# One core, a hybrid S5 and SSD layer: loads of the S5 output tied to gate tiles, and a place of its own for each S5 output block

## Chip, cores and metric

The kernel runs on one core of a Trainium2 chip. The metric is the time of one execution on the device, in microseconds (us). The five engines of the core are named as in the profile: PE (TensorE), DVE (VectorE), ACT (ScalarE), POOL (GpSimd) and SP (SyncE), which here issues all DMAs.

## What is computed

One layer of a streaming encoder, 1024 frames of 1024 channels, in float32. Cut to what matters here:

```python
hn   = rmsnorm(h, norm_w)
proj = hn @ w_in                                   # 1024 x (u | z_s5 | z_ssd | xBC | dt)
u_s5, z_s5, z_ssd, xBC, dt_raw = split(proj)

# S5 branch: 64 groups of 16 channels, 64 complex states each
y    = scan(u_s5) ... + D * u_s5
y    = gelu(y)                                     # "S5 output", Yd in the kernel
y    = y * sigmoid(y @ w_glu + b_glu)              # the GLU: needs all of y at once
y_s5 = y * silu(z_s5)

# SSD branch: 16 heads, state 128, in 8 steps of 128 frames
y    = ssd_chunked(silu(conv(xBC)), dt, A, B, C) + D * xs
g    = y * silu(z_ssd)
y_sd = g * rsqrt(mean(g*g over 256 channels) + EPS) * norm_w

h    = h + concat(y_s5, y_sd) @ w_out
h    = h + (p @ w_ple) * sigmoid(rmsnorm(h) @ w_gate)
out  = rmsnorm(h)
```

## The kernel before

Every large product works on tiles of 128 output channels by 1024 frames. A weight tile comes by one DMA into `wraw`, ACT casts it into `whi` (L138), POOL or DVE makes the remainder `wlo` (L141), and PE then does, for each of 8 slices of the inner dimension, three products (hi x hi, hi x lo, lo x hi) on two halves of 512 frames, so 48 matmuls a tile (`dense`, L162). These weight matmuls are the bulk of the work of PE.

The program order around the change is:

- projections of `u`, with the first parts of the S5 branch (a generator, `s5_chain`) pulled between;
- 16 convolution tiles and 4 gate tiles. The S5 branch goes on between them and ends with `s5_out`: eight blocks of eight channel groups. Block b needs its Toeplitz block `tp` (eight loads of 64 KB from `Kd`, L468), its inputs `ug` (one load from `Ud`, L399) and the rows `CAo` that DVE makes from `cb`. PE does 16 small products into two PSUM tiles, ACT puts the Gelu of each into SBUF (L508), and one DMA stores the block to `Yd` (L509). The loads of block b+1 are written ahead of the products of block b. `tp` and `ug` have two places each;
- 12 gate tiles (`z_tile`: a product, a Silu on ACT, a store to `Zd` in L846). The SSD chain (`ssd_chain`, steps k = 0 to 7) is pulled between and in the middle of them. Among the last eight of these tiles stand the 16 loads that bring the S5 output back as `m_0` to `m_7`, two for each (L874);
- the GLU: all eight `m` are split into hi and lo (L226 has the subtraction), then eight product tiles, each followed by a load of the gate `z` (L886) and the two multiplications; the SSD chain goes on;
- the output projection and what follows.

A step k of the SSD chain loads `csB` (decays, broadcast to 128 partitions, L605) and `cc` (L606), has 16 DVE operations for the decays (L618, eight and eight), and an exponential on ACT; matmuls on `csB` give the step's output; `ys` is multiplied with the gate block `zc` (L681) and squared; the squares are summed over partitions by matmuls with ones: ACT copies the hi part `nh` (L174), DVE subtracts for the lo part `nl` (L175), and PE does one matmul on each (L176, L177). Behind them stand the products with `BT` for the next state (L709) and the scores of the next step (L628).

Three things set the order. Engines execute their own instructions in order. The order in which the instructions of an engine stand is decided by a scheduler when the kernel is built, from the program's dependencies and its estimate of durations; a dependency can also be added by hand that holds for this order alone and puts no semaphore on the chip (`in_line`). And all DMAs stand in SP's queue in one order; besides what it needs, each waits for the DMA eight places ahead of it to have landed.

Of the kernel before, what the change touches and what calls it, by code (L numbers as in the profile page):

```python
# [8 lines left out]
F32 = mybir.dt.float32  # L9
F32R = mybir.dt.float32r  # L10
AF = mybir.ActivationFunctionType
ALU = mybir.AluOpType

P = 128
# [28 lines left out]
ZORD = list(range(8, 16)) + list(range(8))  # L43
# [16 lines left out]
def hybrid_layer(ctx: ExitStack, tc: tile.TileContext, xT, pT, w_in, w_dt, w_glu, w_out, w_gate, w_ple,  # L60
                 prm, cst, bst, cstt, crow, brow, out):
    nc = tc.nc
    V, S, G, T = nc.vector, nc.scalar, nc.gpsimd, nc.tensor
    dma = nc.sync.dma_start
# [34 lines left out]
    Yd = dram.tile([64, 8, 16, P], F32, tag="Yd", name="Yd")  # L99
# [10 lines left out]
    def psa():  # L110
        return ps_a.tile([P, 512], F32, tag="a", name="psa")

    def hf(t, i):
        return t[:, i * 512:(i + 1) * 512]
# [34 lines left out]
    def wnext(ahead=1):  # L149
        wfetch(1)  # L150
        w = wq.pop(0)
        wfetch(ahead)
        return w
# [10 lines left out]
    def dense(wt, rhs, nk=KT, cols=HALVES, bank=psd, mid=None):  # L164
        ps = [bank()[:, :x.stop - x.start] for x in cols]
        for k in range(nk):
            if mid is not None and k == nk // 2:
                mid()
            dense_k(ps, wt, rhs, k, nk, cols)
        return ps  # L170
# [26 lines left out]
    def in_line(ins):  # L197

        for a, b in zip(ins, ins[1:]):
            tc.add_manual_dep(b.ins, a.ins.name, mybir.DependencyInfo(mybir.DependencyClass.NoSync, mybir.DependencyReason.DATA),  # L200
                              reason="in line")

    def evac(ps, dst, func=AF.Copy):
        for h in range(2):
            S.activation(hf(dst, h), ps[h], func)


    def js(ap):
        return ap.rearrange("p (t j s) -> p t s j", j=8, s=16)
# [20 lines left out]
    def pull(gen, n=1):  # L230
        for _ in range(n):
            if next(gen, "end") == "end":
                return False
        return True
# [228 lines left out]
    def load_out(q4, b):  # L463
        cb = q4.tile([P, 2, 8, 16], F32, tag="cb", name="cb")
        dma(cb, crow[:, b])
        tp = q4.tile([P, 8, P], F32, tag="tp", name="tp")
        for s in range(8):
            dma(tp[16 * s:16 * s + 16],  # L468
                Kd[b].rearrange("(g h) c -> h g c", h=16)[:, :, 112 - 16 * s:240 - 16 * s])
        return cb, tp, load_u(q4, b)  # L470

    def s5_out(Er, Ei, wx, q4, ahead):
        with tc.tile_pool(name="q5", bufs=1, side="right") as q5:

            EO = q5.tile([P, 2, 8, 64], F32, tag="EO", name="EO")
            lo_, up = slice(0, 64), slice(64, P)
            for g2, src in enumerate((lo_, up)):
                for r, j, x, sign in ((lo_, 0, Er, 1.0), (lo_, 1, Ei, 1.0), (up, 0, Ei, -1.0), (up, 1, Er, 1.0)):
                    S.activation(EO[r, j, :, g2:64:2], x[src, J0 + 1:J0 + 9], AF.Copy, scale=sign)

            def rows(b, cb):

                CA = q5.tile([P, 8, 8, 16], F32, tag="CAo", name="CAo", bufs=2)
                t = q5.tile([P, 8, 8, 16], F32, tag="cat", name="cat")
                for j, dst in ((0, CA), (1, t)):
                    V.tensor_tensor(dst, cb[:, j, :, None, :].broadcast_to([P, 8, 8, 16]),
                                    EO[:, j, :, 8 * b:8 * b + 8].rearrange("p j g -> p g j")[:, :, :, None].broadcast_to([P, 8, 8, 16]),
                                    ALU.mult)
                V.tensor_tensor(CA.rearrange("p g j c -> p (g j c)"), CA.rearrange("p g j c -> p (g j c)"),
                                t.rearrange("p g j c -> p (g j c)"), ALU.subtract)  # L490
                return CA
            CA = rows(0, ahead[0][0])
            yield
            for b in range(8):
                _, tp, ug = ahead.pop(0)
                if b < 7:
                    ahead.append(load_out(q4, b + 1))
                    nxt = rows(b + 1, ahead[0][0])
                ysb = tp.rearrange("p (q g) c -> p q g c", g=2)
                for g2 in range(2):  # L500
                    yp = psa()
                    for q in range(4):
                        o = yp[:, q * P:(q + 1) * P]
                        g = 2 * q + g2
                        T.matmul(o, tp[:, g, :], ug[:, g, :], start=True, stop=False)  # L505
                        T.matmul(o, CA[:, g].rearrange("p j c -> p (j c)"), wx[:, 8 * b + g].rearrange("p r c -> p (r c)"), start=False, stop=True)  # L506

                    S.activation(ysb[:, :, g2, :].rearrange("p q (s j) -> p q s j", j=8), js(yp), AF.Gelu_apprx_tanh)  # L508
                dma(Yd[8 * b:8 * b + 8].rearrange("g t h c -> (t h) g c"), tp)  # L509
                CA = nxt  # L510
                yield

# [304 lines left out]
    for m in range(8):  # L817
# [5 lines left out]
        else:  # L823
            ps = dense(wnext(), xhl)
# [11 lines left out]
    def z_tile(m, mid=None):  # L836

        z = pz.tile([P, NT], F32, tag="z", name="z")
        ps = dense(wnext(), xhl, mid=mid)
        if m < 8:  # L840
            evac(ps, z, AF.Silu)
        else:
            zk = z.rearrange("p (k t c) -> p t k c", k=8, t=8)
            for h in range(2):
                S.activation(zk[:, 4 * h:4 * h + 4], ps[h].rearrange("p (t k c) -> p t k c", t=4, k=8), AF.Silu)
        dma(Zd[m], z)  # L846


    es_z = ExitStack()
    pz = es_z.enter_context(tc.tile_pool(name="pz", bufs=2))  # L850
    with tc.tile_pool(name="p3", bufs=2) as p3:
        at = {"c": 0, "z": 0}
        for c, n in zip(SEQ, PX):
            m = at[c]
            at[c] += 1
            if c == "c":
                conv_tile(m, p3)
            else:
                z_tile(ZORD[m])
            pull(s5, n)  # L860
# [6 lines left out]
    mt = [mpool.tile([P, NT], F32, tag=f"m_{m}", name=f"m_{m}") for m in range(8)]  # L867
    ssd = ssd_chain()
    for m, n in zip(range(NZ, 16), PZ):
        z_tile(ZORD[m], lambda: pull(ssd, n))  # L870

        for i in range(8)[m - NZ - 4:m - NZ - 3] if m >= NZ + 4 else ():
            for h2 in range(2):
                dma(mt[i][64 * h2:64 * h2 + 64].rearrange("p (t c) -> p t c", t=8), Yd[:, :, 2 * i + h2, :])  # L874
        pull(ssd, n)


# [2 lines left out]
    for m in range(8):  # L880
        ps = dense(wnext(), yhl, mid=lambda: pull(ssd, PG[m]))
# [3 lines left out]
        z = pz.tile([P, NT], F32, tag="z", name="z6")  # L885
# [9 lines left out]
    for m in range(8):  # L895
        dma(h_t[m], xT[m])
        ps = dense(wnext(), mhl, mid=lambda: pull(ssd, PO[m]))
# [8 lines left out]
    with tc.tile_pool(name="npool", bufs=1, side="right") as npool:  # L906
# [10 lines left out]
        for m in range(8):  # L917
            raw = npool.tile([P, NT], F32, tag="raw", name="m2raw", bufs=2).rearrange("p (k c) -> p k c", k=8)
            dma(raw, Sd[:, m].rearrange("k p c -> p k c"))
            t = npool.tile([P, NT], F32, tag=f"m2_{m}", name=f"m2_{m}")  # L920
# [6 lines left out]
    for m in range(8):  # L927
        ps = dense(wnext(1 if m < 7 else 0), m2hl)
# [29 lines left out]
    for m, cols in [(m, HALVES if m < GB else A2) for m in range(8)] + [(m, LASTC) for m in range(GB, 8)]:  # L958
# [9 lines left out]
        for i, c in enumerate(cols):  # L968
            n = c.stop - c.start
# [136 lines left out]
```

## Time and profile before

| | |
|---|---|
| Time, median of 3 runs | 994.84 us (993.02 to 996.24) |
| The profiled execution | 993.96 us, span 992.1 us |
| PE busy | 959.4 us, 97% of the span |
| DVE, ACT, POOL busy | 629.2, 449.5, 212.0 us |
| Moved by DMA | 144.92 MB, mean 146 GB/s |
| Largest waits of PE | 5.4 us for `nh`, 5.0 us for `tp<-Kd` (3 times), 3.3 us for `CA` |
| S5 output stage | about 380 to 445 us of the span |
| The 12 gate tiles with SSD steps | about 445 to 565 us |

PE is the engine that is nearly always busy. What the other engines do costs time where PE waits for it. The time between the span and the profiled execution lies ahead of the first and behind the last instruction.

### The profile page before, as it was taken

To read this page: it belongs to the slowest core of one execution; us is meant where nothing else is said; L and a number is where in the kernel's file an instruction comes from. 1 tells how busy PE (TensorE), PEld (TensorE's weight loads), DVE (VectorE), ACT (ScalarE), POOL (GpSimd) and SP (SyncE) were. 2 spreads that over 40 slices of the span, in tenths; PEclk is the share of its full clock that TensorE was granted. 3 is DMA by queue.
4 is the path that set the end of the run, shared out by engine and by line. 5 is a ranking of instruction groups with operands and counts; after the bars stand their busy time and mean duration, and the time that the engine had idled before them with its cause. 6 is when DMAs were issued, how large, how long until landed. Compare 5 with 4: busy or idle time off the path is not lost.

```text
span 992.1 us, 12846 instructions
## 1 busy us (share of the span) xinstructions
PE 959.4 (97%) x4902; PEld 796.8 (80%) x4902; DVE 629.2 (63%) x983; ACT 449.5 (45%) x586; POOL 212.0 (21%) x150
## 2 busy tenths in 40 slices
PE   8999999989999999989889999999999999999995
PEld 5788777778888888878768888888887888888994
DVE  6599689947998997313467967789511511534436
ACT  8444222357665354334245644565224521463234
POOL 0000000000000032001124255554332373342000
PEclk9999999999999999999979999999999999999997
DMA  8135667296222226879975776566336340020004
GB/s 301 30 99 133 182 203 251 89 209 189 85 107 86 106 85 190 224 212 257 244 242 186 220 201 198 172 199 207 105 113 184 127 144 22 1 69 1 1 1 170
DMA packets 130636, 144.92 MB, mean 146 GB/s; under 512 B 5776, under 2 KB 108176, under 8 KB 129552
## 3 DMA queue, kind: packets, MB, share of 16 engines
q1 hardware_dynamic: 130576, 144.10, 49.1%
q8 instruction: 39, 0.64, 0.3%
q14 instruction: 21, 0.17, 0.1%
HBM read 109.15 MB, written 34.93 MB: 145 GB/s over the span
## 4 chain that ended last, share of the span: by engine, by line
PE 74%; DMA 8%; DVE 7%; SPq 6%; issue 2%; ACT 2%; DVEq 0%; POOL 0%; ACTq 0%; POOLq 0%
PE psd L162 61%; SPq L874 2%; SPq L468 2%; DMA Yd<-tp 2%; PE psa L162 2%; PE psa L672 2%; PE psa L664 1%; PE psa L709 1%; DMA tp<-Kd 1%; PE psa L423 1%; DMA br<-in_brow_dram 1%; PE psa L505 1%; DVE xnlo L812 1%; DMA wraw<-in_w_in_dram 1%; PE psa L506 1%
## 5 line engine op out<-in xcount | busy, mean ns | idle before, releaser
L162 PE MATMUL psd<-xnhi,whi 128*128 128x512 f32 x592 | 187.0, 394 | 0.0
L162 PE MATMUL psd<-xnlo,whi 128*128 128x512 f32 x592 | 184.9, 392 | 0.0
L162 PE MATMUL psd<-xnhi,wlo 128*128 128x512 f32 x592 | 184.4, 391 | 0.2 <-DVE wlo L141 0.2
L141 POOL TENSOR_TENSOR wlo<-wraw,whi 128x1024 fp32r<-128x1024 f32 x44 | 113.0, 2572 | 237.2 <-ACT whi L138 230.5
L138 ACT ACTIVATE whi<-wraw 128x1024 fp32r<-128x1024 f32 x71 | 74.8, 1056 | 180.2 <-PE psd L162 141.3
L162 PEld LDWEIGHTS psd<-xnlo,whi 128*128 128x128 f32 x592 | 110.9, 188 | 24.1 <-DVE xnlo L812 0.9
L162 PEld LDWEIGHTS psd<-xnhi,wlo 128*128 128x128 f32 x592 | 110.7, 188 | 24.3 <-issue 1.0
L162 PEld LDWEIGHTS psd<-xnhi,whi 128*128 128x128 f32 x592 | 110.3, 188 | 23.5 <-issue 1.8
L618 DVE SCALAR_TENSOR_TENSOR csB<-csB,csM,cst_t 128x128 f32<-128x128 f32 x128 | 50.4, 466 | 38.4 <-DMA csB<-Rd 38.4
L593 DVE SCALAR_TENSOR_TENSOR cv<-pad,prm_t,cv 128x1024 f32<-128x1024 f32 x48 | 65.8, 1370 | 8.4 <-ACT cv L591 8.2
L930 DVE TENSOR_TENSOR h<-h,psd 128x512 f32<-128x512 f32 x16 | 10.3, 683 | 63.3 <-PE psd L162 63.3
L162 PE MATMUL psd<-hhi,wlo 128*128 128x384 f32 (+2 forms) x168 | 47.0, 340 | 0.0
L162 PE MATMUL psd<-hlo,whi 128*128 128x384 f32 (+2 forms) x168 | 46.6, 338 | 0.0
L162 PE MATMUL psd<-hhi,whi 128*128 128x384 f32 (+2 forms) x168 | 46.4, 338 | 0.0
L971 DVE TENSOR_TENSOR gt<-psd,rstdB 128x384 f32<-128x384 f32 (+2 forms) x21 | 11.1, 558 | 52.3 <-PE psd L162 42.3
L162 PE MATMUL psd<-yhi,whi 128*128 128x512 f32 x128 | 40.5, 399 | 0.0
L162 PE MATMUL psd<-mhi,wlo 128*128 128x512 f32 x128 | 39.8, 391 | 0.6 <-POOL wlo L141 0.6
L162 PE MATMUL psd<-ylo,whi 128*128 128x512 f32 x128 | 40.2, 393 | 0.0
L162 PE MATMUL psd<-mlo,whi 128*128 128x512 f32 x128 | 39.8, 391 | 0.0
L162 PE MATMUL psd<-yhi,wlo 128*128 128x512 f32 x128 | 39.6, 391 | 0.0
L162 PE MATMUL psd<-mhi,whi 128*128 128x512 f32 x128 | 39.5, 390 | 0.0
L162 PE MATMUL psd<-nhi,wlo 128*128 128x512 f32 x128 | 39.4, 389 | 0.0
(297 smaller groups left out, 1851.4 us busy)
## 6 DMA issues: line engine op xcount, KB each, us to landing
wraw<-in_w_in_dram SPq DMA_DIRECT2D x39, 512.0 KB, 6.0
Cd<-pad SPq DMA_DIRECT2D x16, 512.0 KB, 4.0
Zd<-z SPq DMA_DIRECT2D x16, 512.0 KB, 6.4
ug<-Ud SPq DMA_DIRECT2D x16, 512.0 KB, 4.7
csB<-Rd SPq DMA_DIRECT2D x8, 1024.0 KB, 8.0
cc<-Cd SPq DMA_DIRECT2D x8, 1024.0 KB, 7.5
wraw<-in_w_out_dram SPq DMA_DIRECT2D x16, 512.0 KB, 4.9
Ud<-u SPq DMA_DIRECT2D x16, 256.0 KB, 3.7
```

The costliest lines, as they stand in the source:

```text
L138: S.activation(hi, raw, AF.Copy)
L141: E.tensor_tensor(lo, raw, f(hi), ALU.subtract)
L162: T.matmul(p, w[:, c], rhs[k][r][:, x], start=(k == 0 and j == 0), stop=(k == nk - 1 and j == 2))
L423: T.matmul(xp[:, i * P:(i + 1) * P], wx[:, g + i].rearrange("p r c -> p (r c)"), ug[:, 4 * g4 + i, :], start=True, stop=True)
L468: dma(tp[16 * s:16 * s + 16], Kd[b].rearrange("(g h) c -> h g c", h=16)[:, :, 112 - 16 * s:240 - 16 * s])
L505: T.matmul(o, tp[:, g, :], ug[:, g, :], start=True, stop=False)
L593: conv_last[0] = V.scalar_tensor_tensor(cv, pad[:, d:d + 8, 1:129], pr("convw", 4 * m + d), cv, ALU.mult, ALU.add)
L618: i_ = V.scalar_tensor_tensor(csB[:, h], csB[:, h], csM[:, 16 * k + h:16 * k + h + 1], cap, ALU.subtract, ALU.min)
L672: T.matmul(yp[:, q * P:(q + 1) * P], st[:, h:h + 2].rearrange("p a b -> p (a b)"), cc[:, 12 + 2 * i + q // 2], start=True, stop=True)
L874: dma(mt[i][64 * h2:64 * h2 + 64].rearrange("p (t c) -> p t c", t=8), Yd[:, :, 2 * i + h2, :])
L930: V.tensor_tensor(hf(h_t[m], h), hf(h_t[m], h), ps[h], ALU.add)
L971: first = V.tensor_tensor(gt, pg[i], rstdB[:, c], ALU.mult)
```

## The change

1. `z_tile` returns the last Silu of its tile, and each pair of loads of `m_i` is put, by `in_line`, behind the Silu of the gate tile that it is written after. This binds the order in which the instructions stand and adds no semaphore.
2. The Gelu of an S5 output block goes into a tile of its own, `yo`, with one place, instead of over the Toeplitz block `tp`. The store reads `yo`.
3. To make room for `yo`, `cat` in `rows` has half its size. DVE multiplies and subtracts the second term in two halves: one operation of 1024 elements and four of 512 for a block in place of three of 1024.

```diff
     def evac(ps, dst, func=AF.Copy):
         for h in range(2):
-            S.activation(hf(dst, h), ps[h], func)
+            i_ = S.activation(hf(dst, h), ps[h], func)
+        return i_
...
-                t = q5.tile([P, 8, 8, 16], F32, tag="cat", name="cat")
-                for j, dst in ((0, CA), (1, t)):
-                    V.tensor_tensor(dst, cb[:, j, :, None, :].broadcast_to([P, 8, 8, 16]),
...
+                t = q5.tile([P, 4, 8, 16], F32, tag="cat", name="cat")
...
+                V.tensor_tensor(CA, *bc(0, slice(0, 8)), ALU.mult)
+                fl = lambda x: x.rearrange("p g j c -> p (g j c)")
+                for g in (slice(0, 4), slice(4, 8)):
+                    V.tensor_tensor(t, *bc(1, g), ALU.mult)
+                    V.tensor_tensor(fl(CA[:, g]), fl(CA[:, g]), fl(t), ALU.subtract)
                 return CA
...
-                ysb = tp.rearrange("p (q g) c -> p q g c", g=2)
+                yo = q5.tile([P, 8, P], F32, tag="yo", name="yo")
+                ysb = yo.rearrange("p (q g) c -> p q g c", g=2)
...
-                dma(Yd[8 * b:8 * b + 8].rearrange("g t h c -> (t h) g c"), tp)
+                dma(Yd[8 * b:8 * b + 8].rearrange("g t h c -> (t h) g c"), yo)
...
     for m, n in zip(range(NZ, 16), PZ):
-        z_tile(ZORD[m], lambda: pull(ssd, n))
+        done = z_tile(ZORD[m], lambda: pull(ssd, n))
 
         for i in range(8)[m - NZ - 4:m - NZ - 3] if m >= NZ + 4 else ():
             for h2 in range(2):
-                dma(mt[i][64 * h2:64 * h2 + 64].rearrange("p (t c) -> p t c", t=8), Yd[:, :, 2 * i + h2, :])
+                in_line((done, dma(mt[i][64 * h2:64 * h2 + 64].rearrange("p (t c) -> p t c", t=8), Yd[:, :, 2 * i + h2, :])))
```

The scheduler moves instructions with it. Three places matter. The first is SP in the S5 output stage, blocks 0 to 3, before (the store `Yd<-tp`, then the Toeplitz loads into the place that the store read):

```order
L399 DMA ug<-Ud 128x8x128
L509 DMA Yd<-tp 128x8x128
L465 DMA cb<-in_crow_dram 128x256
L399 DMA ug<-Ud 128x8x128
L509 DMA Yd<-tp 128x8x128
L468 DMA tp<-Kd 16x8x128 x16
L465 DMA cb<-in_crow_dram 128x256
L846 DMA Zd<-z 128x1024
L137 DMA wraw<-in_w_in_dram 128x1024
```

and after:

```order
L469 DMA tp<-Kd 16x8x128 x2
L513 DMA Yd<-yo 128x8x128
L469 DMA tp<-Kd 16x8x128 x6
L400 DMA ug<-Ud 128x8x128
L513 DMA Yd<-yo 128x8x128
L469 DMA tp<-Kd 16x8x128 x8
L400 DMA ug<-Ud 128x8x128
L466 DMA cb<-in_crow_dram 128x256 x2
L850 DMA Zd<-z 128x1024
```

The Toeplitz loads of block 2 moved ahead of and around the first store, and both loads of `ug` moved behind Toeplitz loads: that of block 3 stands behind the second store and all eight loads of its block. On PE, blocks 0 to 7 stood as 2, 2, 1, 1, 1, 1 with weight matmuls between; now they stand as four pairs, with 36, 34 and 34 weight matmuls between.

The second place is SP behind the S5 output stage, where the loads `m<-Yd` begin. Before:

```order
L874 DMA m_0_3271<-Yd_82 64x8x128 x2
L605 DMA csB_3618<-Rd_86 128x2048
L606 DMA cc_3617<-Cd_85 128x16x128
L846 DMA Zd_87<-z_3519 128x1024
L605 DMA csB_3622<-Rd_86 128x2048
L606 DMA cc_3621<-Cd_85 128x16x128
L874 DMA m_1_3272<-Yd_82 64x8x128 x2
L874 DMA m_2_3273<-Yd_82 64x8x128 x2
L644 DMA zc_3742<-Zd_87 128x8x128
L137 DMA wraw_3761<-in_w_in_dram 128x1024
```

and after, from the first step's `csB` on:

```order
L610 DMA cc_3645<-Cd_85 128x16x128
L137 DMA wraw_3696<-in_w_in_dram 128x1024
L617 DMA E0B_3953<-Rd_86 64x8x128 x2
L648 DMA zc_3766<-Zd_87 128x8x128
L879 DMA m_0_3295<-Yd_82 64x8x128 x2
L850 DMA Zd_87<-z_3543 128x1024
L137 DMA wraw_3785<-in_w_in_dram 128x1024
L879 DMA m_1_3296<-Yd_82 64x8x128 x2
L850 DMA Zd_87<-z_3605 128x1024
L137 DMA wraw_3901<-in_w_in_dram 128x1024
L879 DMA m_2_3297<-Yd_82 64x8x128 x2
L850 DMA Zd_87<-z_3695 128x1024
```

The pairs of m loads now stand one to a gate tile, each with a store and a weight between it and the next; the last pair, of `m_7`, stands behind the first load `z<-Zd` of the GLU.

The third place is DVE in the first SSD step (k = 0), where `nl` is made. Before:

```order
L681 TENSOR_TENSOR ys<-ys,zc 128x1024
L175 TENSOR_TENSOR nl<-zc,nh 128x512
L618 SCALAR_TENSOR_TENSOR csB<-csB,csM,cst_t 128x128 x16
L716 COPY st<-psa 128x512
L700 TENSOR_TENSOR ys<-ys,zc 128x1024
```

and after:

```order
L685 TENSOR_TENSOR ys<-ys,zc 128x1024
L622 SCALAR_TENSOR_TENSOR csB<-csB,csM,cst_t 128x128 x16
L175 TENSOR_TENSOR nl<-zc,nh 128x512
L720 COPY st<-psa 128x512 x2
L634 TENSOR_TENSOR csB<-csB,psa 128x512 x2
```

The 16 decay operations (of step k = 2) moved from behind `nl` to ahead of it.

## Rows read from the trace of the kernel before

**Rows 1.** The page, first block: busy us (share of the span) xinstructions of each engine.

```profile
PE 959.4 (97%) x4902; PEld 796.8 (80%) x4902; DVE 629.2 (63%) x983; ACT 449.5 (45%) x586; POOL 212.0 (21%) x150
```

**Rows 2.** Waits of PE, whole span: us in total, times, longest us.

```profile
PE psa L176 <- ACT nh L174: 5.4, 1, 5.4
PE psa L505 <- DMA tp<-Kd: 5.0, 3, 2.0
...
PE psa L423 <- DMA ug<-Ud: 2.5, 1, 2.5
```

**Rows 3.** Windows: stretch, us, busy of PE, PEld, DVE, ACT, POOL, PEclk, DMA share, GB/s.

```profile
220.00:224.00 4.00, 3.17 (x16) 3.20 (x17) 3.14 (x3) 0.59 (x1) 0.00 (x0) 0.57 1.10 337
380.00:445.00 65.00, 60.03 (x382) 53.26 (x382) 23.49 (x20) 22.78 (x31) 7.20 (x3) 1.00 0.83 227
445.00:492.00 47.00, 47.00 (x249) 39.22 (x248) 20.60 (x49) 18.74 (x19) 8.50 (x4) 1.00 1.04 242
492.00:508.00 16.00, 9.38 (x30) 6.99 (x29) 8.60 (x20) 8.76 (x10) 2.36 (x1) 0.68 0.97 317
```

**Rows 4.** PE timeline: start us, us, engine, line, instruction, count [idle before].

```profile
398.65 0.46 PE L505 MATMUL psa<-ug,tp 128*128 128x128 f32 x2 [1.03 <-DMA tp<-Kd]
...
405.79 0.48 PE L162 MATMUL psd<-xnhi,whi 128*128 128x512 f32 x1
...
498.41 0.80 PE L176 MATMUL psa<-nh,ones_r 128*128 128x512 f32 x1 [5.38 <-ACT nh L174]
...
507.19 0.47 PE L162 MATMUL psd<-xnlo,whi 128*128 128x512 f32 x1
...
568.36 0.39 PE L176 MATMUL psa<-nh,ones_r 128*128 128x512 f32 x1
...
571.35 0.70 PE L162 MATMUL psd<-ylo,whi 128*128 128x512 f32 x2
```

**Rows 5.** Chain of waits, 690 to 722 us: start us, us, what.

```profile
707.98 13.16 PE psd L162 x58
```

**Rows 6.** Chain of waits, 486 to 500 us.

```profile
489.24 7.44 DMA wraw<-in_w_in_dram
...
497.75 0.62 ACT nh L174
```

**Rows 7.** SP timeline, 445 to 492 us, and 557: start us, us, issue, count.

```profile
460.52 9.20 SPq L874 DMA_DIRECT2D m<-Yd  x4
...
477.37 10.16 SPq L874 DMA_DIRECT2D m<-Yd  x7
...
491.18 0.40 SPq L605 DMA_DIRECT2D csB<-Rd  x1
...
557.38 0.57 SPq L886 DMA_DIRECT2D z<-Zd  x1
```

**Rows 8.** Landings of `Yd<-tp` (L509), `ug<-Ud` (L399, 330 to 450 us) and `m<-Yd` (L874).

```profile
DMA to landing us min/median/max: 3.4/4.5/5.5
...
DMA to landing us min/median/max: 4.4/5.2/6.1
...
DMA to landing us min/median/max: 3.5/7.1/7.4
```

**Rows 9.** The page, block 6: KB each, median us from issue to landing.

```profile
csB<-Rd SPq DMA_DIRECT2D x8, 1024.0 KB, 8.0
```

**Rows 10.** DVE timeline.

```profile
501.83 4.29 DVE L618 SCALAR_TENSOR_TENSOR csB<-csB,csM,cst_t 128x128 f32<-128x128 f32 x16 [1.00 <-DMA csB<-Rd]
...
526.06 7.47 DVE L618 SCALAR_TENSOR_TENSOR csB<-csB,csM,cst_t 128x128 f32<-128x128 f32 x16
...
567.82 1.21 DVE L226 TENSOR_TENSOR ylo<-m,yhi 128x1024 fp32r<-128x1024 f32 x1
568.95 0.68 DVE L175 TENSOR_TENSOR nl<-zc,nh 128x512 fp32r<-128x512 f32 x1
```

**Rows 11.** ACT timeline, S5 output stage.

```profile
384.07 0.60 ACT L508 ACTIVATE tp<-psa 128x512 f32<-128x512 f32 x1 [0.97 <-PE psa L506]
```

More of the change, by code (lines that the diff above doesn't have):

```diff
@@ L483, in rows @@
                 CA = q5.tile([P, 8, 8, 16], F32, tag="CAo", name="CAo", bufs=2)
-                t = q5.tile([P, 8, 8, 16], F32, tag="cat", name="cat")
-                for j, dst in ((0, CA), (1, t)):
-                    V.tensor_tensor(dst, cb[:, j, :, None, :].broadcast_to([P, 8, 8, 16]),
[L487 to L490, printed above, removed]
+                t = q5.tile([P, 4, 8, 16], F32, tag="cat", name="cat")
+                bc = lambda j, g: (cb[:, j, g, None, :].broadcast_to([P, g.stop - g.start, 8, 16]),
+                                   EO[:, j, :, 8 * b + g.start:8 * b + g.stop].rearrange("p j g -> p g j")[:, :, :, None]
+                                   .broadcast_to([P, g.stop - g.start, 8, 16]))
+                V.tensor_tensor(CA, *bc(0, slice(0, 8)), ALU.mult)
[3 more added lines that the diff above has]
+                    V.tensor_tensor(fl(CA[:, g]), fl(CA[:, g]), fl(t), ALU.subtract)
                 return CA
@@ L840, in z_tile @@
         if m < 8:
-            evac(ps, z, AF.Silu)
+            i_ = evac(ps, z, AF.Silu)
         else:
@@ L844, in z_tile @@
             for h in range(2):
-                S.activation(zk[:, 4 * h:4 * h + 4], ps[h].rearrange("p (t k c) -> p t k c", t=4, k=8), AF.Silu)
+                i_ = S.activation(zk[:, 4 * h:4 * h + 4], ps[h].rearrange("p (t k c) -> p t k c", t=4, k=8), AF.Silu)
         dma(Zd[m], z)
+        return i_
     es_z = ExitStack()
```

## Prediction

> **What bounds the kernel now.** The page's first block says that TensorE is busy for 959.4 us of a span of 992.1 [rows 1], so only time in which TensorE waits, or runs at half its clock, is to be had. I therefore read its waits over the whole span next, and of them the three that this change can touch [rows 2]: 5.4 us once for ACT's `nh`, 5.0 us in three pieces for `tp<-Kd`, the loads of a Toeplitz block, and 2.5 us for a load of `ug`. The windows put a clock beside them [rows 3]: 1.00 all through the S5 output stage (380 to 445 us), where the three pieces lie, though two of them are about 2 us long; 0.57 in the 4 us behind the 2.5 us wait, which costs 4.00 x 0.43 = 1.7 us; and 0.68 in the 16 us around the `nh` wait. There the clock costs 16.00 x 0.32 = 5.1 us.
>
> The same 5.1 follows from instructions [rows 4]. From the matmul on `nh` to the next stretch of unmixed weight matmuls the kernel took 498.41 to 507.19 = 8.78 us; the same point of the next SSD step took 568.36 to 571.35 = 2.99 us at full clock. The first also held three weight matmuls, and 58 of those in 13.16 us [rows 5] are 0.227 us each, so 3.67 us would have been due: 5.1 us lost. Idle and slow clock make 5.38 + 5.1 = **10.5 us**.
>
> The chain of waits names the cause [rows 6]. TensorE waited for `nh`, an ACT copy that stands in ACT's order behind `whi`, the cast of the next weight; that cast waited for `wraw`, issued at 489.24 and landed 7.44 us later. The weight was asked for late, and SP's timeline shows why [rows 7]: the queue sat in the loads `m<-Yd`, 9.20 us for four and 10.16 us for seven. SP issues in order, each DMA waits for the one eight places back to land, and of these 16 each takes a median 7.1 us to land [rows 8], in a stretch where the 16 DMA engines are full (share 1.04, [rows 3]).
>
> **Tying the m loads to the z tiles: +10.5 us, less what is late next.** Each pair of m loads now stands behind the last Silu of its z tile, so in the order of SP a store, a weight, and only then one pair follow one another. The tie is an order without a semaphore, so no engine gets a new wait. The weight of the tile in question no longer stands behind ten m loads (2 + 7 + 1 since the one before it) but behind two, a tile (some 11 us of matmuls, 48 x 0.227) ahead of its use. I count the whole 10.5 us as removed.
>
> Late next is `nl`, the other half of that same sum. On DVE the 16 decay operations on `csB` of step k = 2 now stand ahead of the `nl` of step 0 (they stood behind). Here that `csB` was issued at 491.18 and was there at 501.83, 10.6 us later, in the fullest stretch; the median of its eight loads is 8.0. The 16 operations took 4.29 us at this step and 7.47 at the next [rows 7, 9, 10]. With 0.68 for `nl` itself that makes 13.0 us from the issue at best, 15.6 by this step's own two numbers, 16.2 by the median landing and the longer group. The buffer comes free with step 0's last matmul on `csB`; from there TensorE, by its order in the changed kernel, has 48 weight matmuls (10.9 us), four transposes, four score matmuls and three of the products with `BT` to do, about 13.3 us in all. So TensorE waits between 0 and 2.9 us for `nl`; I take **-1.5**, between the ends, since the long landing had the jam behind it that the change dissolves. At the far end the dip would come back in part: that is in the rivals.
>
> m_7's two loads are moved past everything to the start of the GLU, behind `z<-Zd`. That issue stood at 557.38 and took 0.57 [rows 7]; with the slowest landing of an m load, 7.4, m_7 is there at about 565.4, while the last of the GLU's splits, the one on m_7, started at 567.82 [rows 7, 8, 10]. I cost it at nothing; if that cover were gone, each us later is a us of TensorE's wait at the first GLU product's end.
>
> **The output place `yo`: -1.7 us.** Before, the Gelu overwrote the Toeplitz block that it came from, so the block's place came free only when the store `Yd<-tp` had landed, and the loads of the block after next waited for it: the 5.0 us of [rows 2]. With `yo` those loads need only TensorE's own matmuls. But `yo` has one place, so the Gelu of the second block of a pair waits for the store of the first, and the order on SP puts the next loads behind that second store. All eight blocks now run in pairs with 34 to 36 weight matmuls between, where before the later ones ran singly.
>
> I follow one pair, with time 0 where TensorE ends block b. A block is (405.79 - 398.65) / 2 = 3.57 us [rows 4]; a Gelu half 0.60 [rows 11]; an issue 0.40 [rows 7], and landings are 3.4 / 4.5 / 5.5 us for the store and 4.4 / 5.2 / 6.1 for `ug` (least, median, most) [rows 8]. By medians: Gelu done 0.7, store issued 0.9, landed 5.4. The Gelu of b+1 (matmuls done at 3.6) can only start now: done 6.6, store issued 6.7, landed 11.2. Behind that store stand eight Toeplitz loads, the eighth of which waits for it to land, and behind the eighth `ug` of b+3: issued 11.7, landed 16.9, usable at 17.2. TensorE wants it after 3.57 + 34 x 0.227 + 3.57 = 14.9. It waits **2.3 us**. In the next gap block b+3 is itself later by that wait while the Gelu ahead of it is not, so about 0.4 is left; in the third gap 2.3 again. That is 5.0, as much as the three pieces before. For the clock behind these waits I add one dip at 1.7 (the 2.5 us wait had one, the pieces of about 2 had none): **6.7 against 5.0**.
>
> Both ends: with the least landings `ug` is usable at 14.2, and TensorE waits for nothing (+5.0). With the most it is usable at 20.1: 5.2 + 1.3 + 5.2 = 11.7 us of waits, and two of them as long as the one at `nh`, with its 5.1 each, so 22 (-17). I stay with the medians, because the chain has two stores and one `ug` in a row and three extremes at once are not likely; DMA share is 0.83 there [rows 3], with the same bytes after.
>
> The Trainium skill ("TensorE: Matmul & The Clock Gate", Part 1) calls half clock the array's default, which activity releases and idleness brings back. The 0.57 and 0.68 agree; the 1.00 beside two waits of 2 us shows that short ones go unpunished. If every one of the three waits here brought a dip of 1.7, the sum would be 3.4 us worse, 990.9.
>
> **Small parts, at nothing.** `cat` is halved, so DVE does one pass of 1024 and four of 512 where it did three of 1024: the same elements, two more instructions a block, at most the 1.21 us of a whole pass of 1024 [rows 10]. DVE is busy 23.5 of 65 us there [rows 3], and the work is a block ahead. ACT's order moves `csB`'s exponential one tile forward and drops one table load; ACT is busy 22.8 of 65 and 18.7 of 47.
>
> **Sum.** 10.5 - 1.5 - 1.7 = 7.3. The profiled run took 993.96 (span 992.1 and what lies around it), so 986.7 in that frame. The median of the runs is 994.84, 0.88 above it: **987.5**.
>
> **Rivals.**
> (B) The S5 stage becomes free: landings come near their least, so its waits and dips are about 1 instead of 6.7. For it: the store now goes out with only two loads ahead of it. Against: two store landings in a row. 987.5 - 5.7 = 981.8.
> (C) The one place `yo` eats the gain: waits of 3.5 us in two gaps and 1 in the middle (8), with dips of 2 to 3 each, S5 stage about 15. Then 994.84 - 10.5 + 1.5 + 10 = 995.8, no change. For it: each 1 us more per landing is 3 us on the chain, and a pair needs both. Against: medians.
> (D) **Slower.** The same chain with its landings at the upper end, in every pair: store landing of 5.5 and `ug` of 6.1 make waits of over 5 us, which the kernel has paid with as much again in slow clock. The S5 stage is 22: 994.84 - 10.5 + 1.5 + 17 = 1002.8. It decides from a store and a `ug` landing about 0.7 us over their medians; from there the waits pass 4 us and the gain is gone. For it: eight Toeplitz loads, a store and `ug` now come in one burst. Against: the bytes are the same.
> The Trainium skill ("Perfetto Trace Analysis", Optimization Strategy) says that the same gap repeating on the engine that should be saturated can mean too few buffers; here two rotating places turn into one for the output. (C) and (D) are what that would make of it; the trace before has the repeating gap [rows 2], with another cause.
> (E) The change doesn't do what it says: `nl` or the exponential of `csB` takes the place of `nh`, with wait and dip, so that only the queue is tidier: the 10.5 stay, and the S5 stage costs its 1.7, 996.5. For it: the DMA engines are full there (1.04) whatever the order of the loads. Against: weight and m loads no longer stand in one row.
>
> **How the numbers follow.** Forecast 0.50 (its own range, S5 stage 4 to 11: 984.8 to 991.8), B 0.17, C 0.15, D 0.13, E 0.05. The range 980 to 998 leaves out D and a little of B. A measurement of this kernel can tell 0.3%, 3.0 us, from no change, so faster is under 991.8: most of the forecast and B, 0.65; within: C, E and the forecast's edge, 0.20; slower: D and C's edge, 0.15.
>
> **What would show it.** Right: no wait on `nh` over 1 us and a clock of 1.00 from 480 to 510; `wraw` asked for a tile ahead; waits on `ug` (no longer `tp`) at block 3 and 7 of about 2 us. Wrong: waits in the S5 stage adding up to over 11 or under 4; a wait on `nl` over 3; a wait in the GLU on `ylo`; clock below 1 between 380 and 440 for more than 4 us.

## The result, and the profile after

| | before | after |
|---|---|---|
| time, median | 993.93 us (992.69 to 996.24) | 983.67 us (979.90 to 985.64) |
| ratio, 95% interval | | 0.9878 [0.9842, 0.9914] |
| profiled execution, span | 993.96, 992.1 us | 984.29, 982.5 us |

The changed kernel is faster by 1.2%, some 10 us where 7.3 were forecast, inside the range of 980 to 998. Two more sets of runs of it, beside the experiments, gave 984.29 us, ratio 0.9891 [0.9866, 0.9916], and 982.59 us, ratio 0.9894 [0.9877, 0.9912].

PE's waits over the whole span, after the change (us in total, times, longest):

```profile
PE psa L353 <- DVE CA L390: 4.6, 2, 3.7
PE psa L509 <- DMA ug<-Ud: 3.6, 2, 2.1
...
PE psa L509 <- ACT yo L512: 2.0, 1, 2.0
PE psa L424 <- DMA ug<-Ud: 1.4, 2, 1.1
...
PE psa L176 <- ACT nh L174: 1.2, 1, 1.2
...
PE psa L177 <- DVE nl L175: 0.3, 1, 0.3
```

Against [rows 2], the 5.4 us for `nh` are 1.2, and the 5.0 us for `tp<-Kd` have become 3.6 + 2.0 for `ug` and `yo`. The waits on `CA` and the first `ug` (L424) lie before 230 us, and the two traces have the same order of instructions on every engine up to 374 us; of these waits more below.

The same windows as in [rows 3] (stretch, us, busy of PE, PEld, DVE, ACT, POOL, granted clock, DMA share, GB/s):

```profile
380.00:445.00 65.00, 59.41 (x382) 53.34 (x382) 24.90 (x33) 21.88 (x30) 7.17 (x3) 1.00 0.81 228
445.00:492.00 47.00, 47.00 (x242) 38.99 (x241) 23.19 (x57) 20.44 (x22) 10.90 (x5) 1.00 0.99 267
492.00:508.00 16.00, 16.00 (x81) 13.27 (x81) 10.46 (x22) 9.23 (x9) 4.33 (x2) 1.00 0.57 162
```

The last row is the result in one line: 16.00 of 16.00 us busy at a clock of 1.00, where 9.38 us at 0.68 stood before. Ahead of it the DMA engines were nearly as busy (0.99 against 1.04) and moved more (267 GB/s against 242), so traffic alone does not explain the wait that was there before.

SP's timeline shows what changed instead (start us, us, issue, count). Against [rows 7]:

```profile
466.02 2.03 SPq L879 DMA_DIRECT2D m<-Yd  x2
474.90 0.33 SPq L850 DMA_DIRECT2D Zd<-z  x1
476.41 0.34 SPq L137 DMA_DIRECT2D wraw<-in_w_in_dram  x1
481.49 0.32 SPq L609 DMA_DIRECT2D csB<-Rd  x1
481.86 2.09 SPq L879 DMA_DIRECT2D m<-Yd  x2
```

SP no longer issues without a break: there are gaps between its pieces. The weight is asked for at 476.41, 13 us earlier than before, and `csB` of step 2 at 481.49, ten earlier. On DVE and PE (timelines; idle before an instruction in brackets, where there was any):

```profile
487.89 6.48 DVE L622 SCALAR_TENSOR_TENSOR csB<-csB,csM,cst_t 128x128 f32<-128x128 f32 x16 [3.85 <-DMA csB<-Rd]
494.30 0.68 DVE L175 TENSOR_TENSOR nl<-zc,nh 128x512 fp32r<-128x512 f32 x1
```

```profile
492.88 0.40 PE L176 MATMUL psa<-nh,ones_r 128*128 128x512 f32 x1
...
495.16 0.58 PE L177 MATMUL psa<-nl,ones_r 128*128 128x512 f32 x1
...
559.32 0.50 PE L176 MATMUL psa<-nh,ones_r 128*128 128x512 f32 x1 [1.16 <-ACT nh L174]
```

At step 0 PE waits neither for `nh` nor for `nl`, although `nl` now stands behind the decays. The 1.16 us are at step 2.

The S5 output stage, PE's timeline, the first product of blocks 3, 5 and 7:

```profile
398.81 0.46 PE L509 MATMUL psa<-ug,tp 128*128 128x128 f32 x2 [1.57 <-DMA ug<-Ud]
...
415.89 0.46 PE L509 MATMUL psa<-ug,tp 128*128 128x128 f32 x2 [1.95 <-ACT yo L512]
...
433.06 0.46 PE L509 MATMUL psa<-ug,tp 128*128 128x128 f32 x2 [2.07 <-DMA ug<-Ud]
```

These are 5.6 us, at a clock of 1.00. The row of block 5 names the Gelu, but that had ended at 415.40; its `ug` landed at 415.80, just ahead of the product, as with the other two. The two other profiles of the same kernel have 4.9 and 4.3.

**Where the 9.6 us of span went.** I cut the span at two PE instructions that both kernels have: the first product on `ug` and `tp`, which stands long ahead of the rest of its block, and the fourth matmul on `nh`. PE's timeline before, then after:

```profile
317.90 0.61 PE L505 MATMUL psa<-ug,tp 128*128 128x128 f32 x4
...
597.08 0.39 PE L176 MATMUL psa<-nh,ones_r 128*128 128x512 f32 x1
```

```profile
317.35 0.61 PE L509 MATMUL psa<-ug,tp 128*128 128x128 f32 x4
...
588.14 0.39 PE L176 MATMUL psa<-nh,ones_r 128*128 128x512 f32 x1
```

The middle part took 279.2 us before and 270.8 after: 8.4 of the 9.6 us. Ahead of it 0.6 us were gained and behind it 0.6, by chance as far as the runs tell. I use this **middle stretch** for all that follows; over three profiles of the changed kernel it was 270.8, 268.6 and 269.4, so a single profile tells differences from some 2 us on.

### The profile page after: what moved, and what is told of

It reads as the page before. It is cut to its first block, busy times and chain, and to the rows that moved or that the text cites. A ratio compares the mean times of both kernels' runs of the same rounds, so it can differ in the third digit from the quotient of the medians.

```text
span 982.5 us, 12851 instructions
## 1 busy us (share of the span) xinstructions
PE 956.1 (97%) x4902; PEld 794.9 (81%) x4902; DVE 628.8 (64%) x999; ACT 447.8 (46%) x585; POOL 213.1 (22%) x150
## 4 chain that ended last, share of the span: by engine, by line
PE 75%; DVE 10%; DMA 8%; ACT 2%; issue 2%; SPq 2%; POOL 0%; DVEq 0%; ACTq 0%
PE psd L162 64%; PE psa L162 2%; DMA ug<-Ud 2%; PE psa L668 1%; PE psa L424 1%; PE psa L676 1%; SPq L469 1%; DMA Yd<-yo 1%; PE psa L713 1%; DMA csB<-Rd 1%; DMA m<-Yd 1%; DVE mlo L227 1%; DMA br<-in_brow_dram 1%; DVE xnlo L816 1%; DVE wlo L141 1%
## 5 line engine op out<-in xcount | busy, mean ns | idle before, releaser
L597 DVE SCALAR_TENSOR_TENSOR cv<-pad,prm_t,cv 128x1024 f32<-128x1024 f32 x48 | 63.7, 1327 | 8.4 <-ACT cv L595 8.2
L162 PE MATMUL psd<-nhi,whi 128*128 128x512 f32 x128 | 39.4, 389 | 0.0
```

The source lines that it names most:

```text
L162: T.matmul(p, w[:, c], rhs[k][r][:, x], start=(k == 0 and j == 0), stop=(k == nk - 1 and j == 2))
L597: conv_last[0] = V.scalar_tensor_tensor(cv, pad[:, d:d + 8, 1:129], pr("convw", 4 * m + d), cv, ALU.mult, ALU.add)
```

## The experiments

Ratios are to the kernel before, from runs on the same chip. "S5 waits" are PE's waits at the S5 output blocks, "middle" is the middle stretch, which the expectations call the stretch from the first S5 matmul on the states to the fourth nh matmul.

| kernel | median us | ratio, 95% interval | S5 waits | nh, nl waits, 480 to 600 | middle |
|---|---|---|---|---|---|
| before (profile) | 993.9 | | 5.0 | 5.4, 1.2 | 279.2 |
| changed, again | 984.3 | 0.9891 [0.9866, 0.9916] | 4.9 | 0, 0.4 | 268.6 |
| changed, third time | 982.6 | 0.9894 [0.9877, 0.9912] | 4.3 | 1.1, 0 | 269.4 |
| tie alone | 986.8 | 0.9928 [0.9901, 0.9956] | 4.1 | 1.1, 2.2 | 270.7 |
| tie alone, again | 983.7 | 0.9917 [0.9895, 0.9939] | 4.4 | 0, 1.1 | 269.4 |
| yo alone | 990.4 | 0.9964 [0.9947, 0.9981] | 4.6 | 0, 4.7 | 275.4 |
| m_4 to m_7 tied, no yo | 989.2 | 0.9941 [0.9919, 0.9964] | 4.5 | 1.0, 5.3 | 277.0 |
| yo alone, nl ahead of the decays | 986.2 | 0.9930 [0.9905, 0.9955] | 4.1 | 0, 0.4 | 273.6 |
| two places for yo | 984.6 | 0.9891 [0.9862, 0.9920] | 3.8 | 0, 0 | 267.6 |
| ug ahead of tp | 985.8 | 0.9920 [0.9899, 0.9941] | 6.2 | 0.5, 0.6 | 271.0 |
| two places, stores on ACT's queue | 982.5 | 0.9878 [0.9857, 0.9900] | 4.6 | 0, 0 | 268.3 |
| two places, half of tp on ACT's queue | 981.6 | 0.9883 [0.9864, 0.9901] | 1.8 | 1.1, 0 | 267.0 |
| two places, no ug from block 2 on | 979.8 | 0.9862 [0.9846, 0.9877] | 1.6 | 0, 0 | 265.3 |

**The tie alone.** Everything of the change but `yo` and the halved `cat`:

```diff
-        z_tile(ZORD[m], lambda: pull(ssd, n))
+        done = z_tile(ZORD[m], lambda: pull(ssd, n))
...
-                dma(mt[i][64 * h2:64 * h2 + 64].rearrange("p (t c) -> p t c", t=8), Yd[:, :, 2 * i + h2, :])
+                in_line((done, dma(mt[i][64 * h2:64 * h2 + 64].rearrange("p (t c) -> p t c", t=8), Yd[:, :, 2 * i + h2, :])))
```

> Only the loads of the S5 output are tied to their gate tiles; the Gelu still overwrites the Toeplitz block and cat is whole. Theory (the late weight made the nh wait, and the tie alone removes it): the wait on nh with its slow clock, 10.5 us before, is down to 1.5 or less, the clock is 1.00 from 480 to 510, the three waits on tp<-Kd of 5.0 us in all stay, and the time is within 2 us of the changed kernel, 982 to 986. Rival (both edits are needed, since the place yo lets the last S5 stores leave earlier and so the m loads begin earlier): the wait on nh stays at 4 us or more and the time is 990 or more.

The middle stretch came out as with the whole change, and the window around `nh` (same columns as above) has the clock back:

```profile
492.00:508.00 16.00, 15.53 (x101) 13.04 (x103) 9.53 (x17) 9.08 (x9) 4.32 (x2) 1.00 0.65 180
```

So the tie alone takes away the `nh` wait with its slow clock. The median, 986.8, was a little outside the 982 to 986 expected, so I ran it again beside the changed kernel on one chip:

> The changed kernel a third time, beside the tie alone on one chip. Theory: 982 to 986, and the stretch from the first S5 matmul on the states to the fourth nh matmul 268 to 271 us.

> The tie alone a second time, on the same chip as the changed kernel. Theory (yo does nothing for the time: its S5 stage waits as long as the one before): the two medians lie within 2 us, 982 to 987. Rival (yo does bring some 3 us, as the two medians of different chips, 986.8 and 984.0, would have it): 986 or more, and 2 us or more above the changed kernel beside it.

982.6 and 983.7, 1.1 us apart, with intervals that overlap (0.9894 [0.9877, 0.9912] and 0.9917 [0.9895, 0.9939]). What `yo` adds to the tie lies between nothing and some 4 us and isn't settled by these runs (over all their sets, on different chips, the changed kernel has a mean of 983.3 us in 15 runs and the tie alone 985.6 in 12); in the profiles' middle stretch it is at most half a us on average (269.6 and 270.1). One thing differs there: with the tie alone PE does wait for `nl` at step 0, 0.93 and 1.13 us, since `csB` took 10.0 and 10.2 us from its issue to the first decay, not 6.4.

**yo alone.** The changed kernel with the m loads free:

```diff
-                in_line((done, dma(mt[i][64 * h2:64 * h2 + 64].rearrange("p (t c) -> p t c", t=8), Yd[:, :, 2 * i + h2, :])))
+                dma(mt[i][64 * h2:64 * h2 + 64].rearrange("p (t c) -> p t c", t=8), Yd[:, :, 2 * i + h2, :])
```

> Only the place yo and the halved cat; the loads of the S5 output are free to move as before. Theory (tie alone): SP again has a row of seven to nine m loads between two weights, PE waits 4 to 6 us for nh with half clock behind it, waits in the S5 output stage are 5 to 6 us, and the time is within 3 us of the kernel before, 991 to 996. Rival (yo brings a good part of the gain): 987 or less.

The time fell between the two, and the wait was not on `nh`. SP, then DVE, then PE:

```profile
475.25 3.90 SPq L879 DMA_DIRECT2D m<-Yd  x4
479.25 2.70 SPq L850 DMA_DIRECT2D Zd<-z  x1
482.05 0.38 SPq L137 DMA_DIRECT2D wraw<-in_w_in_dram  x1
484.64 0.32 SPq L850 DMA_DIRECT2D Zd<-z  x1
486.16 0.33 SPq L137 DMA_DIRECT2D wraw<-in_w_in_dram  x1
486.59 0.37 SPq L609 DMA_DIRECT2D csB<-Rd  x1
```

```profile
494.42 4.29 DVE L622 SCALAR_TENSOR_TENSOR csB<-csB,csM,cst_t 128x128 f32<-128x128 f32 x16 [11.17 <-DMA csB<-Rd]
498.63 0.68 DVE L175 TENSOR_TENSOR nl<-zc,nh 128x512 fp32r<-128x512 f32 x1
```

```profile
492.09 0.40 PE L176 MATMUL psa<-nh,ones_r 128*128 128x512 f32 x1
...
499.37 0.80 PE L177 MATMUL psa<-nl,ones_r 128*128 128x512 f32 x1 [4.65 <-DVE nl L175]
```

The m loads begin ten us earlier here (440.09 against 450.55), so their last row is over by 479 and the weight comes in time for `nh`. But `csB` is asked for at 486.59 behind two stores and two weights, where the changed kernel asks at 481.49, as soon as its place is free; it lands at 494.4, and `nl`, behind 16 decays, makes PE wait. That is the forecast's rival (E), met in this half of the change. The ratio, 0.9964 [0.9947, 0.9981], is a gain clear of noise all the same, some 3.6 us; the S5 stage has little part in it (4.6 us of waits against 5.0).

**Only half of the loads tied.** No `yo`, and the tie for `i >= 4` alone:

```diff
-                in_line((done, dma(mt[i][64 * h2:64 * h2 + 64].rearrange("p (t c) -> p t c", t=8), Yd[:, :, 2 * i + h2, :])))
+                ld = dma(mt[i][64 * h2:64 * h2 + 64].rearrange("p (t c) -> p t c", t=8), Yd[:, :, 2 * i + h2, :])
+                if i >= 4:
+                    in_line((done, ld))
```

> No yo; only the loads of m_4 to m_7 are tied to their gate tiles, those of m_0 to m_3 are free. In SP's order the row of m loads ahead of the weight that came late is now two long instead of ten. Theory (the number of loads between two weights makes the weight late): nh does not wait (under 1 us), the same as with all tied, and the stretch from the first S5 matmul on the states to the fourth nh matmul takes 270 to 273 us. Rival (it is the traffic in the DMA engines, which the first four pairs bring forward, or the wait of nl for the decays, that matters): 275 us or more, with a wait on nh or nl of 3 us or more.

The rival won. No row of m loads is left ahead of the weight, and `nh` of step 0 doesn't wait; but PE's timeline has `nl` in its place, with half clock behind it:

```profile
498.67 0.50 PE L177 MATMUL psa<-nl,ones_r 128*128 128x512 f32 x1 [3.61 <-DVE nl L175]
```

SP asked for `csB` at 486.30 there, again behind two stores and two weights. So my reason was too narrow. The row of m loads ahead of a weight is what the kernel before paid for, and with that row gone its wait is gone, but that is not enough: the full tie also puts the load of `csB` of step 2 at the front of the queue at the moment its place is free.

**nl ahead of the decays.** `yo` alone again, with `nl` of step k bound on DVE ahead of the decays of step k + 2:

```diff
+                    if k >= 2:
+                        in_line((nls[k - 2], i_))
...
-                sum_bcast(vp.rearrange("p (g c) -> p g c", g=4), sg, nh, nl)
+                nls.append(sum_bcast(vp.rearrange("p (g c) -> p g c", g=4), sg, nh, nl))
```

> yo alone, loads of m free, and nl put ahead of the 16 decay operations on DVE (the order that the kernel before had). With yo alone PE waited 4.65 us for nl, behind decays whose csB was asked for late, and 6.83 us ran at half clock. Theory (the late loads hit whatever stands in front; nl was only unlucky to stand behind them): without the decays ahead of it nl is done right after nh, that wait and its slow clock go (about 8 us), and the time is 983 to 986, with csB's exponential late by some us without PE waiting for it. Rival (the wait moves on to the next user of the late csB, the products of step 2, or nh itself comes late as before): a wait of 3 us or more stands elsewhere between 480 and 530 us, and the time stays at 988 to 992.

The wait for `nl` went from 4.65 to 0.41 us, and the only other one between 480 and 600 us is of 0.35:

```profile
495.74 0.51 PE L177 MATMUL psa<-nl,ones_r 128*128 128x512 f32 x1 [0.41 <-DVE nl L175]
```

The time, 986.2, is just outside the 983 to 986 of the theory and outside the rival's. The middle stretch, 273.6, holds two stretches of 3.41 us at half clock behind S5 waits, 1.7 us each; without them it would be 270.2, that of the changed kernel. So for this wait, with the m loads untied, order on DVE does what the order on SP does with the tie: either `csB` is early, or `nl` doesn't stand behind it.

**The S5 output stage.** Five kernels asked what the waits of the pairs hang on.

```diff
-                yo = q5.tile([P, 8, P], F32, tag="yo", name="yo")
+                yo = q5.tile([P, 8, P], F32, tag="yo", name="yo", bufs=2)
```

> The changed kernel with two places for yo; SP's order of the S5 output stage is the same but for one piece near its end. Theory (the one place makes the Gelu of the second block of a pair wait for the first store, 2 us later than its matmuls end, and SP's next loads stand behind that store): the three waits of 1.6 to 2.1 us at blocks 3, 5 and 7 (5.6 us in all) fall to 1.5 or less in all, and the time is 4 to 5 us below the changed kernel, about 979. Rival (the burst of loads in DMA bounds the pairs, whatever the place): the waits stay at 4 us or more in all and the time is that of the changed kernel, 984.

```diff
+        ug = load_u(q4, b)
         tp = q4.tile([P, 8, P], F32, tag="tp", name="tp")
...
-        return cb, tp, load_u(q4, b)
+        return cb, tp, ug
```

> The changed kernel, with one place for yo, but the load of ug is written ahead of the eight Toeplitz loads of its block. Theory of the chain as forecast (two store landings and the landing of ug behind one another): with ug ahead the chain is one store, the second Gelu, the issue of seven Toeplitz loads and the landing of the last of them, about 13.5 us after the block's end against 13.6 to 14 due, so the waits fall from 5.6 us to 2 or less and the time to 979 to 981. Rival (it is the single place alone, ug's position does not matter): waits stay at 5 us or more, 984.

Two places brought the waits from between 4.3 and 5.6 us down to 3.8, less than expected, and the time didn't move beyond its interval. `ug` ahead of `tp` didn't lessen them: the waits passed to the Toeplitz loads, 5.5 us in all, and to the Gelu, 0.8. But the scheduler also put 30, 29 and 28 weight matmuls between the pairs in place of 36, 34 and 34, so the loads were due 1.1 to 1.4 us earlier (0.227 us each), and this run doesn't tell whether the chain got shorter.

```diff
-                dma(Yd[8 * b:8 * b + 8].rearrange("g t h c -> (t h) g c"), yo)
+                nc.scalar.dma_start(Yd[8 * b:8 * b + 8].rearrange("g t h c -> (t h) g c"), yo)
```

> The changed kernel with two places for yo, and the stores of the S5 output issued from ACT's queue, right behind the Gelu, instead of from SP's. With two places alone the waits at blocks 3, 5, 7 only fell from 5.6 to 3.8 us, since the second store of a pair still stood in SP's queue among 20 loads. Theory (SP's queue, its issue times and its eight DMAs in flight, bounds a pair): with the stores gone from it the last ug of a pair is issued 1.5 to 3 us earlier, the waits are 1.5 or less in all, and the stretch from the first S5 matmul on the states to the fourth nh matmul is 265 to 267 us (267.6 with two places alone). Rival (the DMA engines' transfer time bounds the burst): waits stay at 3 us or more.

```diff
-            dma(tp[16 * s:16 * s + 16],
+            (dma if s < 4 else nc.scalar.dma_start)(tp[16 * s:16 * s + 16],
```

> The changed kernel with two places for yo, and four of the eight Toeplitz loads of every block issued from ACT's queue; the bytes are the same, SP issues 14 DMAs for a pair instead of 22. Theory (SP's queue bounds a pair): waits in the S5 output stage 1 us or less in all, the stretch from the first S5 matmul on the states to the fourth nh matmul 265 to 267 us. Rival (the DMA engines' transfers bound it, as the waits of 4.6 us with the stores off SP suggest): waits of 3 us or more in all, landings of ug still over 4 us, the stretch 268 us or more.

> The changed kernel with two places for yo and without the loads of ug of blocks 2 to 7, which use those of blocks 0 and 1 again (so the S5 branch of those groups has wrong inputs). That is 3.1 of some 15.4 MB and one issue of eleven less in the stage. The scheduler then puts 26 to 28 weight matmuls between the pairs instead of 34, so the loads are due 1.8 us earlier. Theory of transfers: the Toeplitz loads' landings fall by a fifth or more and the waits, though due earlier, are 3 us or less in all; DMA share of the stage falls below 0.75. Theory of SP's queue: 10 issues of 11 are left, the waits rise to 5 us or more since the loads are due earlier.

The three have two places for `yo`. In the last, blocks 2 to 7 use the `ug` of blocks 0 and 1. Windows of 380 to 440 us, first the changed kernel, then two places, stores on ACT's queue, half of `tp` on ACT's queue, no `ug`:

```profile
380.00:440.00 60.00, 54.41 (x360) 49.19 (x360) 24.90 (x33) 19.18 (x27) 4.76 (x2) 1.00 0.83 229
```

```profile
380.00:440.00 60.00, 56.19 (x371) 50.84 (x371) 27.64 (x36) 18.87 (x27) 5.25 (x3) 1.00 0.86 232
```

```profile
380.00:440.00 60.00, 55.44 (x369) 50.09 (x368) 26.93 (x36) 18.90 (x26) 4.78 (x2) 1.00 0.89 224
```

```profile
380.00:440.00 60.00, 58.24 (x374) 52.12 (x373) 24.23 (x32) 22.21 (x30) 7.17 (x3) 1.00 0.92 233
```

```profile
380.00:440.00 60.00, 58.38 (x382) 52.54 (x381) 27.63 (x36) 22.17 (x30) 7.12 (x3) 1.00 0.77 211
```

Taking the stores off SP did not lessen the waits (4.6 us against 3.8, with the DMA share up). That is what the rival expected, but the run doesn't test SP's queue cleanly: the scheduler put 43 weight matmuls ahead of the first pair in place of 36, and the stores still held SP up. SP's waits there, 378 to 440 us (us in total, times, longest):

```profile
SPq L469 <- DMA Yd<-yo: 2.2, 1, 2.2
```

The last of eight Toeplitz loads on SP waited 2.2 us, up to 412.9, for the store that ACT's queue had issued at 407.08, though it needs nothing of it: the store still stood among the eight DMAs that may be under way, as far as the trace tells. The `ug` behind that load is the one that PE waited 2.95 us for.

Taking half of the Toeplitz loads off SP brought the waits to 1.8, between theory and rival, with the same bytes, the highest DMA share and landings no shorter (medians: Toeplitz loads 5.0 us against 4.6 with two places alone, `ug` 5.1 against 4.2). PE's timeline there:

```profile
397.29 0.46 PE L509 MATMUL psa<-ug,tp 128*128 128x128 f32 x2 [0.30 <-ACT yo L512]
...
429.97 0.46 PE L509 MATMUL psa<-ug,tp 128*128 128x128 f32 x2 [1.29 <-DMA ug<-Ud]
```

But here too the scheduler moved the pairs. The second stretch between two pairs, weight matmuls alone (stretch, us, busy of PE and count, granted clock, DMA share, GB/s), with two places alone and then with half of `tp` on ACT's queue:

```profile
405.08:412.90 7.82, 7.82 (x34) 1.00 1.07 274
```

```profile
400.85:409.11 8.26, 8.26 (x36) 1.00 0.97 249
```

It is 38, 36 and 36 weight matmuls in place of 36, 34 and 34, so each pair's loads are due 0.45 us later, some 1.4 of the 2.0 us that the waits fell. From the end of a pair to the landing of the last `ug` it took 12.7, 11.8 and 13.6 us, against 13.4, 11.7 and 13.6. So most of what this version gains is time to wait, not a shorter chain, and that SP's row of Toeplitz issues bounds a pair isn't shown. Leaving `ug` out gave 1.6 us of waits, although the loads were due 1.8 us earlier, and the Toeplitz loads landed in a median of 2.9 us in place of 4.6; the DMA share, 0.77, stayed a little over the 0.75 expected. Of its two theories only the one of transfers allows that, but `ug` was also the last link of the chain, so this run doesn't part the two. How much of the chain is issue and how much transfer stays open. None of these versions that compute the whole layer is faster than the changed kernel beyond the intervals: the stores on ACT's queue have 0.9878 [0.9857, 0.9900] against 0.9891 [0.9866, 0.9916] on the same chip, half of `tp` on ACT's queue 0.9883 [0.9864, 0.9901] against 0.9894 [0.9877, 0.9912]. The Trainium skill ("Perfetto Trace Analysis", Optimization Strategy) says that a gap that repeats on the engine that should be saturated can mean too few buffers; here one more place took 0.5 to 1.8 us of it and left 3.8.

**The changed kernel again.**

> The changed kernel as it is, for a second profile and for times on the chip of the runs beside it. If the early waits (on CA and on ug, before 230 us, with or without a stretch at half clock) scatter from run to run and have nothing to do with the change, they differ again here, while from the first S5 matmul on the states to the fourth nh matmul it takes 270 to 272 us as in the first profile (270.8; before 279.2). Rival: that stretch differs by more than 2 us between two profiles of one kernel, and then profiles of single runs can't be compared to a us. Time 982 to 987.

The early waits did differ: on `CA`, at some 135 us of the span, 3.75, 3.50 and 2.18 us in the three profiles, and on `ug`, at some 224 us, 1.10 us with no half clock behind it in one and 1.86 with it in another. The middle stretch was 268.6, 2.1 us under the first profile's, just where the rival begins.

## Why the prediction was right

**The wait on nh, 10.5 us.** Right, and so was the reason as far as the kernel before goes: the weight came late because SP sat in a row of m loads, and with the tie it was asked for 13 us earlier. Wait and slow clock are gone at step 0. The forecast had `csB` of step 2 asked for as soon as its place is free, and took that for given; the half tie shows that it is a second thing that the full tie does. With half of the loads tied the first was cured and the second appeared.

Of the 10.5 the sum is right, but not its parts. The 5.1 us of slow clock were taken from the window, 16.00 x 0.32, which counts half clock while PE stood idle too, and again from 8.78 - 3.67, where the 8.78 us hold a wait for `nl`. PE's timeline before:

```profile
500.88 0.79 PE L177 MATMUL psa<-nl,ones_r 128*128 128x512 f32 x1 [1.24 <-DVE nl L175]
```

So the slow clock cost some 3.9 us, and 5.38 + 1.24 + 3.9 make the 10.5; that both ways gave 5.1 is chance. With this the middle stretch adds up: 10.5 gained, 1.2 lost to `nh` at step 2 and 0.6 in the S5 stage, 8.7, where 8.4 was measured.

**nl, -1.5.** The sum came out by luck (1.2 us on `nh` and 0.3 on `nl`), the place didn't. At step 0 `nl` cost nothing: `csB` landed 6.4 us after its issue, not 8.0 to 10.6; the decays took 6.48, near the long end, and `nl` ended about 0.2 us before PE came to it. Why `csB` landed so soon stays open: with the tie alone SP asked for it as promptly, it took 10.0 and 10.2 us, and PE waited for `nl` much as forecast. The 1.2 us are a wait on `nh` at step 2, which the forecast didn't have; by its own sign (no wait on `nh` over 1 us) that is a miss, in two of three profiles (1.16, 1.10, none).

**The S5 output stage, 6.7 against 5.0.** The mechanism was the forecast one. Timelines of ACT and SP at the second pair:

```profile
405.31 1.09 ACT L512 ACTIVATE yo<-psa 128x512 f32<-128x512 f32 x2 [7.41 <-DMA Yd<-yo]
```

```profile
398.91 0.47 SPq L513 DMA_DIRECT2D Yd<-yo  x1
399.43 4.89 SPq L469 DMA_DIRECT2D tp<-Kd  x6
404.36 0.43 SPq L400 DMA_DIRECT2D ug<-Ud  x1
406.42 0.38 SPq L513 DMA_DIRECT2D Yd<-yo  x1
406.90 4.67 SPq L469 DMA_DIRECT2D tp<-Kd  x8
411.61 0.43 SPq L400 DMA_DIRECT2D ug<-Ud  x1
```

The Gelu of the second block waits for the first store to land; behind it follow the second store, eight Toeplitz loads and `ug`, which landed 4.2 us later, at 415.8, and PE had waited 1.95 us. The sizes were off one by one: waits of 1.57, 1.95 and 2.07 where 2.3, 0.4 and 2.3 were forecast, so that their sum, 5.6, is near the 5.0 is luck. In the middle one the store went out 1.0 us after its Gelu, behind two Toeplitz loads on SP, and its landing released the next Gelu 6.4 us after its issue, not 4.5; in the pair before, behind two as well, it was 3.6, so why it landed late stays open. The dip of 1.7 did not come in any of the three profiles. The term was 6.7 and measured 5.6, 4.9 and 4.3: `yo` costs and gains next to nothing in this stage, since one wait per store is replaced by another.

**The terms at nothing.** No profile of the changed kernel has a wait of PE on `ylo` in the GLU or on `CAo`, so `m_7` and the halved `cat` cost nothing that shows.

**The sum.** 7.3 forecast for the profiled execution, 9.7 measured (993.96 to 984.29): 1.1 of the difference is the S5 term; the rest lies ahead of and behind the middle stretch, by chance as far as the runs tell. The median, 983.67, is 1.1 us under the forecast's own range (984.8 to 991.8), toward the time of rival (B), 981.8. But a free stage, (B), is not what happened: the stage kept its waits. Nor did (C) and (D), longer chains with slow clock.

## What to carry to other kernels

A queue that issues in order turns a row of loads that nobody needs yet into a wait for whoever is next behind it, and what is next changes with the row: look for the loads issued ahead of the late one, and then at what the queue brings late once they are gone. Tying such loads to steps of the program, in the schedule alone, cost nothing that shows here and gave all of the gain that could be told apart. A buffer of its own helps only if the wait doesn't reappear at that buffer: count the landings in a row before adding one. And where an edit also moves what the scheduler puts between, a wait says little by itself: read when the load is due as well as when it lands.

## What the runs showed of the hardware

Whether a short wait of PE is followed by half clock (a granted clock of 0.50, 1.2 of 2.4 GHz) differs from run to run; the forecast's reading, that short ones go unpunished, was too strong. In the `yo`-alone kernel with `nl` ahead a wait of 2.03 us at 433.27 was followed by 3.41 us at half clock, in the changed kernel 2.07 us at 433.06 was not. Windows of the first, then of the second:

```profile
430.00:440.00 10.00, 7.97 (x51) 7.55 (x50) 0.00 (x0) 1.93 (x4) 0.00 (x0) 0.83 0.38 108
```

```profile
430.00:440.00 10.00, 7.93 (x56) 7.18 (x56) 0.00 (x0) 2.52 (x4) 0.00 (x0) 1.00 0.53 151
```

With stores on ACT's queue a wait of 2.95 us had none, and with `ug` ahead of `tp` one of 3.00; with two places for `yo` one of only 1.25 us, at 759.77, had 3.41 us at half clock behind it. The eight waits of 3.25 to 5.38 us in the kernels run here all had such a stretch, of 3.41 to 10.24 us. With PE busy throughout, 3.41 us at half clock cost 1.7, so the waits around 2 us, of which the kernel has some in every profile, may be a part of why runs of one kernel lie up to 6 us apart; no run shows that by itself. The Trainium skill ("TensorE: Matmul & The Clock Gate", Part 1) has idleness bring half clock back; the eight long waits agree, the shorter ones are a matter of the run.
